# A two-layer decoder trunk on one core: scores of two heads in one bank, half projections with two banks, products of zeros ahead of three waits

## The chip, the core and the metric

The kernel runs on one core of a Trainium2 chip. TensorE (PE in the rows; its weight loads are PEld) multiplies, VectorE (DVE), ScalarE (ACT) and GpSimd (POOL) do the elementwise work, SyncE (SP) issues the loads. TensorE's clock is granted at one of two levels, 1.2 or 2.4 GHz; the profile prints the granted clock of a stretch as a share of 2.4 GHz, so 0.50 is the lower level throughout. The metric is device time in microseconds (us) of one execution; the kernel before has a median of 691.52 us over 3 runs (688.81 to 693.57).

## The reference, cut to what matters

256 tokens of width 1024 go through two layers, each a mixer and a squared-ReLU MLP (1024 to 4096 and back) with residual adds and RMSNorms, then a last RMSNorm. The change is in the second mixer, native sparse attention with 16 heads in 4 key/value groups; with 256 tokens every 64-token block is selected and the window covers all, so both of the branches below are causal attention over their own keys:

```python
q, k_c, v_c, k_s, v_s, k_w, v_w, gl = split(h @ w_in)     # h = rms_norm(x)
gates = sigmoid(gl)                                       # 16 heads x 3 branches
kc_blk, vc_blk = compress_blocks(k_c), compress_blocks(v_c)   # silu(blk @ w1) @ w2, 15 blocks
p_c = masked_softmax(q @ kc_blk.T);    o_c = p_c @ vc_blk
p_s = masked_softmax(rope(q) @ rope(k_s).T);  o_s = p_s @ v_s
p_w = masked_softmax(rope(q) @ rope(k_w).T);  o_w = p_w @ v_w
out = (g0 * o_c + g1 * o_s + g2 * o_w) @ w_out
x = x + out;  x = x + squared_relu(rms_norm(x) @ w_up) @ w_down
```

## The kernel before, in words

**Layout.** Activations lie as features x tokens: `X` is 128 x 8 x 256. Products are made at better than half precision by splitting both factors into a rounded part and a rest: a weight piece `st` (128 x 1024 or 128 x 560) is loaded, ScalarE rounds it into `uh`, VectorE subtracts to get `ul`, and every 128 x 128 block takes three products of 256 columns (`mm256`). Weights stream through 8 staging slots and 4 pairs of `uh`/`ul`.

**Order of the work.** Nothing here is left to a compiler's scheduler. Every piece of work is a Python generator that yields the engine, bank, flag or token that it wants next; the class `Order` keeps a clock for each engine and, at every step, lets the generator go on whose next instruction could start first by its own table of costs. The result is one fixed list of instructions for each engine, and on the chip each engine runs its list strictly in order. So a change of costs, banks or tile shapes anywhere in a stretch reorders that stretch on all engines.

**PSUM.** There are 8 banks of 128 x 512 floats. A generator that asks for a bank holds it until the evacuation has read it.

**The second mixer** (`layer1`) runs, by `ORDER1`, the key projection `kk` (tiles `KD`, `KL`), the first half of the queries `q0`, the keys of the compressed branch `kc`, the per-token projection `vg` (values and gates; the rows `b<-uh,x` and `b<-ul,x` with 280 columns), the compression `cmp` (rows `b<-st,blk`, fp32), the queries `q1` and the output projection `wo` (rows `b<-ohl,uh` and `b<-ohl,ul`). The head work is done in 8 units, called **pairs 0 to 7** here, each for two heads of two groups: `q0` brings pairs 0 to 3, `q1` pairs 4 to 7. A pair goes through

- `attend`: the rotary embedding and the split of the queries on VectorE and ScalarE (tiles `swq`, `qrot`, `qr`), then on TensorE the scores: for token block t=0 256 columns a head, for t=1 512 columns a head, each as a product with `KD`, one with `KL` and a mask product (`ngeb`). A head's scores have a bank of their own, four banks in all.
- `soften`: the maximum on VectorE (`nm`), the exponentials on ScalarE (`px`); `weigh` divides and gates them (`px<-px,den`).
- `turn` and `spread` (called by `combine`): TensorE transposes the weights (`b<-par,px`), they are copied out (`pts`) and multiplied with the values (`b<-pts,VT`); the compressed branch is added (`b<-pct,VCB`) and the sum split into `ohl`, which the output projection reads. The flag `o7` says that pair 7 is done.

`proj_tok` (line 612) makes all four 280-column accumulators of `vg` at once in four banks. `proj_out` (line 627) takes four banks at its start, goes through six of the eight feature blocks `k` with 24 products each as the `ohl` come, and finishes the last two block by block. `Norm.finish` (line 745) ends a norm: a sum over partitions on TensorE, a reciprocal root on VectorE, two transposes of a column.

The helper `call` (line 303) issues every engine instruction but DMAs, so nearly all rows name line 303; tiles tell them apart.

## Time and profile before

| | |
|---|---|
| median of 3 runs | 691.52 us |
| the profiled execution | 692.06 us, span 690.3 us |
| PE busy | 664.9 us, 96% of the span |
| PEld, DVE, ACT, POOL busy | 91%, 68%, 57%, 18% |
| mean granted clock | 0.985 |
| the chain that ended last | PE 81%, DVE 12%, ACT 3% |
| loads | 109.08 MB, 158 GB/s in the mean |

PE counts as busy while a product is under way, at either clock and however far its products lie apart, so 96% does not say that PE works at its full rate in 96% of the span. For that, the products in a stretch are counted against the distance at which the same kind of product starts in a stretch where PE waits for nothing. In the timeline a row gives start, duration, engine, operation and, in brackets, the idle time before it with the instruction that ended it; the ends of products are modelled, so the distance of two starts is the better price than the duration.

### The profile page before, as it was taken

To read this page: it belongs to the slowest core of one execution; us is meant where nothing else is said; L and a number is where in the kernel's file an instruction comes from. 1 tells how busy PE (TensorE), PEld (TensorE's weight loads), DVE (VectorE), ACT (ScalarE), POOL (GpSimd) and SP (SyncE) were. 2 spreads that over 40 slices of the span, in tenths; PEclk is the share of its full clock that TensorE was granted. 3 is DMA by queue.
4 is the path that set the end of the run, shared out by engine and by line. 5 is a ranking of instruction groups with operands and counts; after the bars stand their busy time and mean duration, and the time that the engine had idled before them with its cause. 6 is when DMAs were issued, how large, how long until landed. Compare 5 with 4: busy or idle time off the path is not lost.

```text
span 690.3 us, 16239 instructions
## 1 busy us (share of the span) xinstructions
PE 664.9 (96%) x6629; PEld 626.2 (91%) x6629; DVE 466.4 (68%) x869; ACT 392.7 (57%) x766; POOL 125.2 (18%) x172
## 2 busy tenths in 40 slices
PE   8999899999999999999999989998999999999994
PEld 5999799989999999999999847895799999999994
DVE  6999777686765565555589976895696565555452
ACT  7565232245887885444457566666588887644430
POOL 1001766311200000010122630030130000011121
PEclk9999999999999999999999979999999999999997
DMA  8861533135666666666644528140145555555401
GB/s 293 297 225 33 156 96 93 52 113 174 187 201 192 193 199 190 193 198 192 190 147 133 184 88 279 62 153 31 62 153 184 187 202 192 189 204 189 153 1 62
DMA packets 32330, 109.08 MB, mean 158 GB/s; under 512 B 3712, under 2 KB 3968, under 8 KB 32256
## 3 DMA queue, kind: packets, MB, share of 16 engines
q1 hardware_dynamic: 31968, 107.53, 49.2%
q8 instruction: 52, 0.85, 0.5%
q10 hardware_dynamic: 288, 0.52, 0.2%
q14 instruction: 22, 0.18, 0.1%
HBM read 106.99 MB, written 1.05 MB: 157 GB/s over the span
## 4 chain that ended last, share of the span: by engine, by line
PE 81%; DVE 12%; ACT 3%; issue 2%; DMA 1%; SPq 0%; DVEq 0%; ACTq 0%
PE b L303 81%; DVE ul L303 4%; DMA X<-xt 1%; ACT uh L303 1%; DVE nm L303 1%; DVE cvconv L303 1%; DVE kc L303 1%; DVE swq L303 1%; DVE rqt L303 1%; DVE lc L303 0%; ACT E L303 0%; DVE x L303 0%; SPq L435 0%; DVE preconv L303 0%; DVE al L303 0%
## 5 line engine op out<-in xcount | busy, mean ns | idle before, releaser
L303 DVE TENSOR_TENSOR ul<-st,uh 128x1024 fp32r<-128x1024 f32 (+3 forms) x204 | 242.1, 1190 | 153.1 <-ACT uh L303 150.9
L303 ACT ACTIVATE uh<-st 128x1024 fp32r<-128x1024 f32 (+3 forms) x204 | 206.1, 1012 | 199.1 <-PE b L303 179.0
L303 PE MATMUL b<-x,uh 128*128 128x256 f32 x1664 | 294.5, 280 | 1.6 <-ACT uh L303 0.9
L303 PEld LDWEIGHTS b<-x,uh 128*128 128x128 f32 x1664 | 251.8, 188 | 5.2 <-ACT uh L303 2.0
L303 PE MATMUL b<-x,ul 128*128 128x256 f32 x832 | 231.2, 278 | 1.2 <-DVE ul L303 1.1
L303 PE MATMUL b<-U,uh 128*128 128x256 f32 x1024 | 174.2, 276 | 0.0
L303 PEld LDWEIGHTS b<-x,ul 128*128 128x128 f32 x832 | 156.4, 188 | 2.4 <-DVE ul L303 2.4
L303 PEld LDWEIGHTS b<-U,uh 128*128 128x128 f32 x1024 | 154.1, 188 | 0.0
L303 PE MATMUL b<-U,ul 128*128 128x256 f32 x512 | 141.3, 276 | 0.0
L303 PEld LDWEIGHTS b<-U,ul 128*128 128x128 f32 x512 | 96.1, 188 | 0.0
L303 POOL TENSOR_TENSOR nacc<-nacc,sq 128x256 f32<-128x256 f32 x24 | 28.4, 1182 | 251.4 <-ACT sq L303 248.7
L303 ACT ACTIVATE px<-b,nm 128x128 f32<-128x128 f32 (+1 forms) x64 | 26.2, 422 | 7.6 <-DVE nm L303 7.5
L303 ACT ACTIVATE U<-u 128x256 fp32r<-128x256 f32 x64 | 26.8, 419 | 2.0
L303 ACT ACTIVATE u<-t 128x256 f32<-128x256 f32 x64 | 26.7, 418 | 2.0
L303 DVE TENSOR_TENSOR U<-u,U 128x256 fp32r<-128x256 f32 x64 | 27.0, 424 | 0.9 <-ACT U L303 0.9
L303 PE MATMUL b<-uh,x 128*128 128x264 f32 (+1 forms) x128 | 25.3, 291 | 0.0
L303 POOL TENSOR_TENSOR px<-px,den 128x128 f32<-128x128 f32 x32 | 15.1, 500 | 54.5 <-DVE den L303 53.6
L303 PE MATMUL b<-ohl,uh 128*128 128x256 f32 x128 | 24.0, 287 | 0.2
L303 POOL TENSOR_TENSOR X<-X,par 128x256 f32<-128x256 f32 x8 | 5.5, 693 | 99.3 <-ACT nacc L303 90.3
L303 ACT ACTIVATE t<-b 128x256 f32<-128x256 f32 x64 | 23.4, 365 | 0.0
L303 ACT ACTIVATE pts<-b 128x384 f32<-128x384 f32 x26 | 12.2, 490 | 17.6 <-PE b L303 17.5
L303 DVE TENSOR_REDUCE nm<-b 128x2 f32<-128x256 f32 (+1 forms) x32 | 16.6, 549 | 6.1 <-PE b L303 6.0
(269 smaller groups left out, 797.0 us busy)
## 6 DMA issues: line engine op xcount, KB each, us to landing
st<-wts SPq DMA_DIRECT2D x188, 512.0 KB, 4.1
st<-wts SPq DMA_DIRECT2D x8, 280.0 KB, 2.8
st<-wts SPq DMA_DIRECT2D x8, 264.0 KB, 5.9
st<-wts SPq DMA_DIRECT2D x8, 256.0 KB, 6.3
X<-xt SPq DMA_DIRECT2D x3, 256.0 KB, 6.4
par<-par SPq DMA_DIRECT2D x1, 525.0 KB, 5.8
out_dram<-X SPq DMA_DIRECT2D x2, 256.0 KB, 2.6
out_dram<-X ACTq DMA_DIRECT2D x2, 256.0 KB, 3.1
```

Of the source, the lines that this page charges most:

```text
L303: r = f(*a, **k)
```

## The change

Six edits; the first mixer, both MLPs and the loads keep their instructions.

1. **Scores of t=0 share a bank.** Both heads of a pair write 2 x 256 columns of one bank, only the first product clears it, and `soften2` takes one maximum over 512 columns instead of `soften`'s two over 256. t=1 keeps two banks.
2. **`KL` gets 128 rows.** It had, for each head, 64 rows (the rounding rest of the head's keys); now the other 64 rows are zeros, set once by two POOL memsets, and the product runs over all 128 rows of `qr`. The column counts are the same.
3. **`vg` in halves** (`proj_tok2`): the first 280 columns for both token blocks with two banks, then the second 280. The weight array is laid out to match; bytes and products are the same.
4. **`wo` in halves** (`proj_half`, since `HALF[1]` is 1): output features 0 to 511 with two banks over all eight `k`, then 512 to 1023 with two. It asks for its first bank only once the flag `o0` is up.
5. **Products of zeros** (`keep`): where the planner's clock sees PE idle for more than `KEEP` = 900 ns ahead of a pair's scores, a turn or the last norm's two products, it issues up to 8 products of a tile of zeros (128 x 512, bf16) into the bank that the waiting work is about to clear.
6. The 9 products at the start of the program become 11, on the same tile of zeros.

```diff
+WARM, KEEP, KMAX = 11, 900.0, 8
+ONE, WO, HALF, SOFT, TURN, VH = 1, 0, (0, 1), None, None, 1
...
+    def keep(bank):
+
+        gap = order.idle('PE', bank)
+        if gap > KEEP:
+            n = min(int((gap - 400) / 215), KMAX)
+            for _ in range(n):
+                nc.tensor.matmul(bank, e.zeros[:, :128], e.zeros, start=True, stop=True)
...
+    def proj_tok2(norm, half, finish):
+
+        for b in range(2):
+            accs = yield from banks(2)
+            for k in range(KT):
+                if k % 2 == 0:
+                    hi, lo = yield from unit()
+                yield 'flag', f'n{norm.idx}x{k}'
+                s = slice(k % 2 * half, k % 2 * half + half)
+                for t in range(2):
+                    yield 'PE'
+                    xt = norm.x[:, k, :, t * 128:t * 128 + 128]
+                    mm256(accs[t][:, :half], xt[:, 0], xt[:, 1], hi[:, s], lo[:, s], k == 0, k == KT - 1)
+            spawn(finish(accs, b))
...
+    def proj_half(x, ready, nxt):
...
+        for half in range(2):
+            accs = yield from banks(2)
...
+            for k in range(KT - 2):
+                yield from ready(k)
+                if k % 2 == 0:
+                    u = yield from unit()
+                for m in range(4):
+                    yield 'PE'
+                    piece(k, m, u)
+            for k in (KT - 2, KT - 1):
+                yield from ready(k)
+            u = yield from unit()
+            for m in range(4):
+                for k in (KT - 2, KT - 1):
+                    yield 'PE'
+                    piece(k, m, u)
+                if m % 2:
+                    spawn(evac(4 * half + m, accs[m // 2]))
...
             yield 'PE'
+            if self.last:
+                keep(ss)
...
-        KL = p1.tile([128, 2, 2, T], F32R, name="KL")
+        KL = p1.tile([128, 2, 2, 2, T], F32R, name="KL")
...
+            for s in range(2):
+                yield 'G'
+                G.memset(KL[64 - 64 * s:128 - 64 * s, s].bitcast(F32), 0.0)
+            flag('KL')
...
-                bk = yield from banks(2)
-                sc = [view(b, 2, n) for b in bk]
+                one = ONE and not t
+                if one:
+                    b = yield BANK
+                    bk, sc = [b, b], [view(b, 2, 2, n)[:, s] for s in range(2)]
+                else:
+                    bk = yield from banks(2)
+                    sc = [view(b, 2, n) for b in bk]
                 q = slice(t * 128, t * 128 + 128)
                 yield 'PE'
+                e.keep(bk[0])
                 for s in range(2):
-                    PE.matmul(sc[s], qr[:, s, q], KD[:, s, p, :, :n], start=True, stop=False)
+                    PE.matmul(sc[s], qr[:, s, q], KD[:, s, p, :, :n], start=not (one and s), stop=False)
                 yield 'PE'
                 for s in range(2):
-                    PE.matmul(sc[s], qr[own[s], s, q], KL[own[s], p, :, :n], start=False, stop=False)
+                    PE.matmul(sc[s], qr[:, s, q], KL[:, s, p, :, :n], start=False, stop=False)
...
+        def soften2(u, bank, PX, nm, den):
+
+            sc = view(bank, 2, 2, 128)
+            yield 'V'
+            V.tensor_reduce(nm[:, 0], sc, axis=AX.X, op=OP.max, negate=True)
...
+        yield 'flag', f'o{WO}'
+        yield from (e.proj_half if HALF[1] else e.proj_out)(lambda k: [ohl[k // 2][:, a, k % 2] for a in range(2)], ready, nxt)
```

The planner's list moves between the key projection and the start of the second MLP; before and behind that, only the 2 + 10 products of zeros at the two ends of the program are new. Three places matter for what follows.

TensorE's list, where the per-token projection ends and the scores of the next pair begin. Before, pairs 0 and 1 have had their scores among the `vg` products; then come four compression products, pair 2 and pair 3:

```order
L303 MATMUL b_5467<-uh_5569,x 128x280
L303 MATMUL b_5721<-st,blk_4976 64x256
L303 MATMUL b_5721<-st,blk_4977 64x256
...
L303 MATMUL b_5730<-KD,qr 128x256
L303 MATMUL b_5731<-KD,qr 128x256
L303 MATMUL b_5730<-KL,qr 128x256
...
L303 MATMUL b_5754<-KD,qr 128x256
```

The same place now; pair 0 has had its scores ahead of `vg`, and no score stands among the `vg` products:

```order
L314 MATMUL b_5584<-uh_5593,x 128x280
L420 LDWEIGHTS zeros
L420 MATMUL b_5690<-zeros 128x512
L314 MATMUL b_5690<-KD,qr 128x256 x2
L314 MATMUL b_5690<-KL,qr 128x256 x2
...
L314 MATMUL b_5709<-KD,qr 128x256 x2
...
L314 MATMUL b_5743<-st,blk_4978 64x256
...
L314 MATMUL b_5758<-par,px_0_5430 128x128
L314 MATMUL b_5758<-par,px_0_5431 128x128 x2
```

So two products of zeros, pairs 1 and 2, six compression products and then the first transposes follow the last `vg` product; pair 3's scores have moved behind 30 of the 32 compression products.

VectorE's list behind its last `ul` of `vg` (`ul_5570` before). Before, the query work of pairs 1, 2 and 3 alternates with maxima (`nm`) of scores that TensorE has yet to make:

```order
L303 TENSOR_TENSOR ul_5570<-st,uh_5569 128x560
L303 TENSOR_TENSOR kc<-b_5421,rbc 64x128 x2
L303 TENSOR_REDUCE nm<-b_5545 128x2
L303 STREAM_SHUFFLE swq<-QQ 128x256
...
L303 TENSOR_REDUCE nm<-b_5575 128x2
L303 TENSOR_REDUCE nm<-b_5608 128x2
L303 TENSOR_TENSOR qr<-qrot,qr 64x256 x2
...
L303 TENSOR_REDUCE nm<-b_5680 128x2
L303 TENSOR_REDUCE nm<-b_5681 128x2
L303 TENSOR_TENSOR qr<-qrot,qr 64x256 x2
L303 CAST qr<-qrot 64x256
```

Now pair 0's maxima lie ahead of the last `ul`, and the query work of pairs 1 and 2 follows it in one piece, `x4` being both pairs' halves:

```order
L314 TENSOR_TENSOR ul_5594<-st,uh_5593 128x560
L314 TENSOR_TENSOR kc<-b_5419,rbc 64x128 x2
L314 STREAM_SHUFFLE swq<-QQ 128x256
L314 TENSOR_TENSOR swq<-swq,rtab 128x256
L314 TENSOR_TENSOR qrot<-qrot,swq 128x256
...
L314 CAST qr<-qrot 64x256
L314 TENSOR_TENSOR qr<-qrot,qr 64x256 x4
L314 TENSOR_SCALAR gate<-gate 128x96
L314 TENSOR_REDUCE nm<-b_5690 128x4
```

TensorE's list at the end of the attention, where pair 7 is combined. Before, 144 of the 192 output products stand ahead of this place, 48 behind it:

```order
L303 MATMUL b_6748<-par,px_2_6466 128x128
L303 MATMUL b_6748<-par,px_2_6467 128x128 x2
L303 MATMUL b_6321<-ohl_6592,uh_6424 128x256 x2
...
L303 MATMUL b_6794<-pts,VT 64x128 x2
L303 MATMUL b_6794<-pct,VCB_4971 128x256
L303 MATMUL b_6318<-ohl_6804,uh_6474 128x256 x2
```

Now 72 stand ahead of it, since the second half may not begin before the first has ended, and 120 behind:

```order
L314 MATMUL b_6308<-ohl_6518,uh_6276 128x256 x2
L314 MATMUL b_6308<-ohl_6518,ul_6277 128x256
L314 MATMUL b_6689<-par,px_3_6562 128x128
...
L314 MATMUL b_6688<-pts,VT 64x128 x2
L314 MATMUL b_6688<-pct,VCB_4973 128x256
L314 MATMUL b_6307<-ohl_6709,uh_6321 128x256 x2
```

So the attention of pairs 5 to 7 has half as many output products among its own, and a longer tail of them follows.

## Rows read from the trace of the kernel before

**Rows 1.** Windows by stage: length, busy us (count) per engine, granted clock, DMA

```profile
core 0: us, PE busy (x) PEld busy (x) DVE busy (x) ACT busy (x) POOL busy (x), PEclk, DMA share, GB/s
354.40:379.80 25.40, 25.40 (x224) 25.40 (x225) 23.62 (x43) 17.51 (x34) 7.79 (x7) 1.00 0.40 122
379.80:397.70 17.90, 17.27 (x122) 14.91 (x121) 16.93 (x42) 10.29 (x30) 11.31 (x20) 1.00 0.51 177
397.70:413.20 15.50, 13.24 (x56) 6.25 (x55) 11.63 (x31) 9.21 (x38) 5.55 (x12) 0.67 0.23 72
413.20:450.30 37.10, 37.10 (x305) 29.63 (x304) 27.45 (x75) 24.53 (x72) 4.25 (x6) 1.00 0.49 169
450.30:502.60 52.30, 48.34 (x362) 39.47 (x361) 37.21 (x89) 30.11 (x88) 10.23 (x20) 0.97 0.25 81
502.60:514.80 12.20, 11.61 (x99) 11.16 (x97) 11.47 (x14) 9.85 (x19) 5.42 (x5) 1.00 0.56 171
```

**Rows 2.** Timeline of TensorE, from the end of `vg` to the first transposes

```profile
398.04 1.08 PE L303 MATMUL b<-st,blk 128*64 128x256 f32 x8 [0.33 <-issue]
400.96 0.81 PE L303 MATMUL b<-KD,qr 128*128 128x256 f32 x2 [1.84 <-DVE qr L303]
...
409.07 3.68 PE L303 MATMUL b<-st,blk 128*64 128x256 f32 x16
412.68 0.64 PE L303 MATMUL b<-par,px 128*128 128x128 f32 x3
```

**Rows 3.** Timeline of VectorE, behind the last `ul` of `vg`

```profile
388.99 1.13 DVE L303 TENSOR_TENSOR ul<-st,uh 128x560 fp32r<-128x560 f32 x1
390.16 0.60 DVE L303 TENSOR_TENSOR kc<-b,rbc 64x128 f32<-64x128 f32 x2
...
391.25 0.45 DVE L303 STREAM_SHUFFLE swq<-QQ 128x256 f32<-128x256 f32 x1
...
392.54 1.28 DVE L303 TENSOR_REDUCE nm<-b 128x2 f32<-128x512 f32 x2
393.85 0.87 DVE L303 TENSOR_TENSOR qr<-qrot,qr 64x256 fp32r<-64x256 f32 x2
```

**Rows 4.** Timeline of TensorE, prices at full clock: compression, transposes, products with the values

```profile
422.75 0.65 PE L303 MATMUL b<-st,blk 128*64 128x256 f32 x4
423.34 0.87 PE L303 MATMUL b<-par,px 128*128 128x128 f32 x6
424.14 1.91 PE L303 MATMUL b<-pts,VT 128*64 128x256 f32 x16
```

**Rows 5.** Timeline of TensorE, the scores of pair 4 and the start after them

```profile
443.22 0.39 PE L303 MATMUL b<-KD,qr 128*128 128x256 f32 x2
...
444.00 0.71 PE L303 MATMUL b<-KD,qr 128*128 128x512 f32 x2
444.65 0.50 PE L303 MATMUL b<-KL,qr 64*128 64x512 f32 x2
445.08 0.39 PE L303 MATMUL b<-ngeb,identb 128*128 128x256 bf16 x2
445.31 0.98 PE L303 MATMUL b<-KCB,QQ 128*128 128x32 f32 x8
```

**Rows 6.** Timeline of TensorE, waits in the attention of pairs 5 to 7 and behind it

```profile
468.68 0.52 PE L303 MATMUL b<-par,px 128*128 128x128 f32 x3 [2.35 <-ACT px L303]
...
511.92 0.39 PE L303 MATMUL b<-x,uh 128*128 128x256 f32 x1 [0.46 <-DVE x L303]
```

**Rows 7.** Timeline of GpSimd, the rotary table of the second mixer

```profile
355.33 1.31 POOL L303 TENSOR_TENSOR rope<-rtab,rbc 128x512 f32<-128x512 f32 x1 [7.62 <-ACT rbc L303]
```

**Rows 8.** Timeline of TensorE, start of the program and the last norm

```profile
1.22 4.02 PE L303 MATMUL b<-warm 128*128 128x512 bf16 x9 [1.22 <-DVE warm L303]
...
10.61 0.50 PE L303 MATMUL b<-x,uh 128*128 128x256 f32 x2 [0.75 <-ACT uh L303]
...
683.08 0.69 PE L303 MATMUL b<-par,ncol 128*128 128x128 f32 x2 [1.82 <-DVE ncol L303]
```

More of the change, by code (lines that the diff above doesn't have):

```diff
@@ L75, in _layout @@
     eo = i['ev_w_out'][0].reshape(2, 4, 128, 1024)
-    for h in (1, 0):
-        chunks.append(eo[h].transpose(1, 0, 2).reshape(128, CH))
+    if HALF[0]:
+        a = eo[::-1].reshape(8, 128, 2, 512).transpose(2, 1, 0, 3)
+        chunks.extend(a.reshape(2, 128, CH))
+    else:
+        chunks.extend(eo[h].transpose(1, 0, 2).reshape(128, CH) for h in (1, 0))
     def mlp(l):
@@ L101, in _layout @@
     wo = i['od_w_out'][0].reshape(2, 2, 4, 64, 1024).transpose(2, 0, 1, 3, 4).reshape(1024, 1024)
-    part['wo'] = [h.transpose(1, 0, 2).reshape(128, CH) for h in wo.reshape(2, 4, 128, 1024)]
+    part['wo'] = [h.transpose(1, 0, 2).reshape(128, CH) for h in
+                  (wo.reshape(8, 128, 2, 512).transpose(2, 0, 1, 3) if HALF[1] else wo.reshape(2, 4, 128, 1024))]
     for k in ORDER1:
@@ L225, in spend, with idle @@
         c.last = eng
+    def idle(self, eng, bank):
+        c = self.cur
+        start = max(c.hold + self.IN[eng], c.t + self._lag(c, eng))
+        return start - max(self.free[eng], self.since[id(bank)] + self.IN[eng])
     def later(self, ns):
@@ L398, in _build @@
     ones = const.tile([128, 1], F32, name="ones")
+    e.zeros = const.tile([128, 512], BF16, name="zeros")
+    def keep(bank):
[4 more added lines that the diff above has]
+                nc.tensor.matmul(bank, e.zeros[:, :128], e.zeros, start=True, stop=True)
+            at = int(order.free['PE'] / TICK)
+            order.cols[at] = order.cols.get(at, 0.0) + n * 512
+    e.keep = keep
     def begin():
@@ L766, in finish @@
             yield 'PE'
+            if self.last:
+                keep(rb)
             for t in range(2):
@@ L1426, in ready @@
                 yield 'flag', 'ya1'
-        yield from e.proj_out(lambda k: [y[:, k % 4] for y in (yb if k < 4 else ya)], ready, nxt)
+        yield from (e.proj_half if HALF[0] else e.proj_out)(lambda k: [y[:, k % 4] for y in (yb if k < 4 else ya)], ready, nxt)
 def layer1(e, n, nxt):
@@ L1666, in attend @@
                     PE.matmul(sc[s][:, :, n - 128:], e.identb, e.ngeb[:, None, :].to_broadcast([128, 2, 128]),
-                              start=False, stop=True)
-                    spawn(soften(u, s, t, bk[s], sc[s], PX, nm, den))
+                              start=False, stop=not one or s == 1)
+                    if not one:
+                        spawn(soften(u, s, t, bk[s], sc[s], PX, nm, den), SOFT)
+                if one:
+                    spawn(soften2(u, bk[0], PX, nm, den))
             give('qr')
@@ L1681, in soften @@
             flag(f'px{u}.{s}{t}')
+        def soften2(u, bank, PX, nm, den):
+            sc = view(bank, 2, 2, 128)
+            yield 'V'
+            V.tensor_reduce(nm[:, 0], sc, axis=AX.X, op=OP.max, negate=True)
+            for s in range(2):
+                for b in range(2):
+                    yield 'A'
+                    A.activation(PX[0][:, s, b], sc[:, s, b], AF.Exp, bias=nm[:, 0, s, b:b + 1],
+                                 accum_out=den[:, 0, s, b:b + 1])
+                flag(f'px{u}.{s}0')
+            release(bank)
         def weigh(i, p, PX, den):
@@ L1866, in ready @@
             yield 'flag', f'o{k}'
-        yield from e.proj_out(lambda k: [ohl[k // 2][:, a, k % 2] for a in range(2)], ready, nxt)
+        yield 'flag', f'o{WO}'
+        yield from (e.proj_half if HALF[1] else e.proj_out)(lambda k: [ohl[k // 2][:, a, k % 2] for a in range(2)], ready, nxt)
 def kernel(**inputs):
```

57 lines of the change are left out of this document (42 added, 15 removed).

## The prediction

> **What bounds the kernel now.** I began with the windows by stage, because 96% PE busy hides more than it tells. [rows 1] Outside the second mixer PE starts a 256-column product every 25.40/224 = 0.113 us and waits for nothing; there the change alters nothing, so its worth is read between 379.8 and 514.8 us. I count each stage's products at the distance of their starts in undisturbed stretches: a pair's scores 445.31 - 443.22 = 2.09 us [rows 5]; a compression product (423.34 - 422.75)/4 = 0.148 us, a transpose (424.14 - 423.34)/6 = 0.133 us, a value product 1.91/16 = 0.119 us [rows 4].
>
> - The per-token stage, 17.90 us, is 0.63 us short of busy and holds two pairs' scores (4.2), so its 96 products took (17.90 - 0.63 - 4.2)/96 = 0.136 us each, 13.1 in all.
> - The 15.50 us behind it hold 28 compression products (4.1), two pairs (4.2) and three transposes (0.4): 8.7 us of work, **6.8 us lost**. Its granted clock is 0.67, the lowest of the table.
> - 413.2 to 450.3 us is full, at clock 1.00: nothing to win.
> - The output stage, 52.30 us: 192 products (21.8), three pairs (6.3), 48 transposes (6.4), 64 value products (7.6), and 20 small ones at a transpose's price (2.7), 44.8 us; **7.5 us lost**, 4.0 of it open idle time.
> - The first 96 products of the second MLP: 12.20 us for 10.9, **1.3 us lost**.
>
> The timeline of TensorE shows how the 6.8 us go [rows 2]: `vg` ends, eight compression products fill one us, PE waits 1.84 us for the `qr` of pair 2, and then the clock is at its lower level until the transposes: pairs 2 and 3 with four compression products take 409.07 - 400.96 = 8.1 us, where 4.2 + 0.6 would do. `qr` is late because VectorE is nearly full (16.93 of 17.90 us [rows 1]) and its list puts query work behind maxima [rows 3].
>
> **The change, part by part.**
>
> *Order around `vg` and the compression.* Pair 0's scores come first, so `vg` starts 2.1 us later, at 381.9, and without other scores among its products ends at 381.9 + 13.1 = 395.0. VectorE's last `ul` ended at 390.1; counting both lists from the rotary table on with the traced durations puts it 0.4 later, at 390.5. Then come a `kc` couple (0.60), the query work of pairs 1 and 2 in one piece, 392.54 - 391.25 = 1.29 each [rows 3], a cast (at most half of the 0.87 for two halves, 0.43) and two `qr` halves (0.87): pair 1 is ready at 390.5 + 0.6 + 2.6 + 0.4 + 0.9 = 395.0, pair 2 at 395.9. PE's wait shrinks from 2.2 us to about 0.5, and the clock has no long idle stretch to fall in. From there to the start of the work that followed 413.2 the same products are due, two pairs at 4.2 instead of 8.1 less 0.6. What is late next: the copies of the first transposes, on ScalarE behind pair 1's exponentials and on VectorE behind pair 3's query work; PE waits about 0.9 us for them in my walk through the three lists. Of 0.63 + 6.8 = 7.4 us lost, 1.4 stay: **-6.0**. Bounds: -7.4 (no wait is left) and -1 (the clock falls all the same).
>
> *Shared bank.* One maximum over 512 columns (1.28/2 = 0.64 us [rows 3]) for two over 256, on VectorE, saves less than one of 0.64 a pair; it is in the walk.
>
> *`KL` over 128 rows.* At t=1 the two 64-row products take 445.08 - 444.65 = 0.43 us, the two full `KD` products of the same width 444.65 - 444.00 = 0.65 [rows 5]. If full rows cost what `KD` costs, 8 pairs pay 8 x 0.22 = **+1.8**; the lower bound is 0. I take the upper, being nearest in shape. The Trainium skill's page "TensorE: Matmul & The Clock Gate" (Part 3: Packing small matmuls) says that products on different rows of the array run at once; filling the rows gives that up, which speaks against this edit. By that rule t=0, half as wide, would lose half as much too, and the term would be +2.7. The two memsets stand ahead of `rope`, where POOL was idle for 7.62 us [rows 7]: nothing, unless they take longer than that.
>
> *`vg` in halves.* Products and bytes are the same, two banks are free earlier: 0 beyond the walk.
>
> *`wo` in halves.* Before pair 7 is combined, 72 output products instead of 144 are at hand; the other 72 x 0.113 = 8.2 us move behind it. In exchange four banks fewer are tied up, and the scores of a pair's t=1 follow its t=0 directly. Walked through with traced durations, pairs 4 to 7 leave PE waiting about 1.0 us for pair 4's weights, 1.6 for copies behind exponentials on ScalarE, 0.9 for pair 5's weights and 2.0 in smaller pieces: 5.5 against 7.5 lost now, **-2.0**, bounds -5 and +6 (three quarters of the 8.2 turn into waits). The wait of 2.35 us for `px` [rows 6] is what this trades against. Behind it `X` of the first half is ready 96 products before the end, 10.9 us early, so the MLP's first products no longer wait for `x` (0.46 of the 1.3 [rows 6]; the rest was slowed): **-1.3**, bounds -1.3 and 0.
>
> *Products of zeros.* At the start they cost 4.02/9 = 0.45 us each [rows 8]; two stand before pair 1 inside its wait, two more at the start are paid back at the first wait behind them (0.75 us [rows 8]) but for 0.15. At the end, five lie in a gap of 1.82 us [rows 8]: 5 x 0.45 = 2.25 would delay the two transposes by 0.4, and if their clock is held they gain up to 0.3. Taken as 0.
>
> Sum: -6.0 + 1.8 - 2.0 - 1.3 = -7.5, from the profiled execution's 692.06 to 684.6. That execution lies 0.5 over the median of 691.52, so the median to expect is **684.1**.
>
> **The rivals.**
>
> *The clock falls anyway.* The `keep` rule acts where the planner sees idle time, not where the chip has it; only two products stand in the mixer. If VectorE is later than counted by 1.5 us, PE idles 2 us at 395 as it does now at 399, and pairs 1 and 2 run at the lower clock: 8.1 - 4.8 = +3.3, twelve compression products at (412.68 - 409.07)/16 = 0.23 us [rows 2] instead of 0.148, +1.0, and the wait itself 0.5: 689. For: VectorE's durations swing when POOL works beside it. Against: query work now stands in one piece.
>
> *Starved attention.* Half of the 8.2 us becomes waiting: instead of -2.0 it is +4, 690. For: lists run strictly in order, and the wait of 2.35 us arose with twice the filler. Against: 2 banks more.
>
> *Slower than before.* The starved attention also loses the clock. From pair 5's transposes to pair 7's end PE has some 20 us of work (two pairs' scores 4.2, 36 transposes 4.8, 48 value products 5.7, 36 output products 4.1, small ones). At the lower clock work took 8.1/4.8 = 1.7 times as long [rows 2]: +14, and with the -2.0 not had, 700. It decides once more than about 18 us of that work runs at the lower level. Against: the output stage had a wait of 2.35 us and still a granted clock of 0.97 [rows 1], 3 us of low clock at most. [...]
>
> *Upside.* All waits of both stages vanish: -7.4 - 5 - 1.3 + 1 = -12.7, near 679.
>
> **How the numbers follow.** What a measurement of this kernel tells from no change is about 1%, 6.9 us: faster is below 684.6, slower above 698.4. The forecast has 0.62 and spreads over 680.5 to 687.5, six tenths of it below 684.6; the upside 0.07; the fallen clock 0.16; starved attention 0.09; slower 0.06, nearly all of it over 698.4. So faster is 0.62 x 0.6 + 0.07 = 0.44, slower 0.05, the same 0.51. A range of 679.5 to 691.0 leaves out the slower case, the worse part of the starved one and the best of the upside.
>
> **What would show it.** In the profile after: the granted clock of the compression stage near 1.00 instead of 0.67, and a wait of under 1 us before the second pair's scores; the t=1 `KL` products at the distance of the `KD` ones; waits for `px` and `pts` between the output products' start and pair 7, 5 to 6 us in sum; 120 output products in a row, and no wait for `x` behind them; the last transposes no later than now. The prediction is wrong if the clock drops at the same place, if the sum of waits in the output stage exceeds 8 us, or if a stage that I hold for unchanged moves.

## The result, and the profile after

The changed kernel has a median of 683.39 us over 4 runs (682.36 to 683.91), the kernel before on the same chip 692.55 over 4 (688.81 to 695.13): a ratio of 0.987, 95% interval 0.9821 to 0.9919. 684.1 had been forecast. The two sums agree better than their terms do, and the terms are what this part is about.

The windows by stage of the changed kernel, to be read against [rows 1]: the per-token stage, pairs 1 and 2 with the compression, the stretch to the first output product, the output stage, the entry of the MLP.

```profile
core 0: us, PE busy (x) PEld busy (x) DVE busy (x) ACT busy (x) POOL busy (x), PEclk, DMA share, GB/s
380.28:397.54 17.26, 16.03 (x123) 15.24 (x121) 16.42 (x40) 11.65 (x33) 7.97 (x14) 1.00 0.48 158
397.54:416.35 18.81, 17.08 (x131) 10.84 (x129) 16.51 (x38) 13.14 (x45) 9.50 (x18) 1.00 0.59 188
416.35:446.97 30.62, 30.26 (x245) 26.15 (x245) 26.23 (x75) 19.05 (x61) 2.71 (x6) 1.00 0.39 146
446.97:496.29 49.32, 47.14 (x362) 39.23 (x361) 38.13 (x87) 30.93 (x91) 12.71 (x21) 1.00 0.28 86
496.29:508.50 12.21, 12.21 (x110) 12.21 (x109) 9.55 (x23) 9.01 (x18) 3.92 (x3) 1.00 0.56 180
```

The granted clock is 1.00 in every row; before it was 0.67 in one stage and 0.97 in another. PE still has open waits in four of the rows, and VectorE is still nearly full in the per-token stage (16.42 of 17.26 us).

To see where the time went, I took starts of TensorE's products that stand at the same place of both programs: the second norm's sum, the last product of the first MLP, the first output product, the first and the last product of the second MLP. In the kernel before they are at 181.95, 346.17, 450.33, 502.62 and 678.89 us; in the timeline of the changed one:

```profile
183.98 0.58 PE L314 MATMUL b<-ones,nacc 128*128 128x1 f32 x4 [0.30 <-DVE nacc L314]
348.15 0.28 PE L314 MATMUL b<-U,ul 128*128 128x256 f32 x1
446.97 0.39 PE L314 MATMUL b<-ohl,uh 128*128 128x256 f32 x2
496.29 0.39 PE L314 MATMUL b<-x,uh 128*128 128x256 f32 x2
671.00 0.28 PE L314 MATMUL b<-U,ul 128*128 128x256 f32 x1
```

| stretch between these starts, us | before | after | difference | forecast |
|---|---|---|---|---|
| start to the second norm (first mixer) | 181.95 | 183.98 | +2.03 | 0 |
| first MLP | 164.22 | 164.17 | -0.05 | 0 |
| second mixer to the first output product | 104.16 | 98.82 | -5.34 | -6.0 + 5/8 x 1.8 = -4.9 |
| output stage | 52.29 | 49.32 | -2.97 | -2.0 + 3/8 x 1.8 = -1.3 |
| second MLP | 176.27 | 174.71 | -1.56 | -1.3 |
| from there to the end of the span | 11.41 | 11.10 | -0.31 | 0 |
| span | 690.3 | 682.1 | -8.2 | -7.5 |

The first row is no work of the change. In the first mixer, whose instructions are the same, TensorE stands still for longer, 2.62 us instead of 1.81, and the granted clock from 84 to 95 us is 0.84 instead of 1.00. The timeline of TensorE before:

```profile
86.27 0.25 PE L303 MATMUL b<-tt,al 32*32 32x32 f32 x4 [1.81 <-issue]
```

After:

```profile
86.72 0.32 PE L314 MATMUL b<-tt,al 32*32 32x32 f32 x6 [2.62 <-issue]
```

The wait is put down to "issue": nothing that the profile shows released it. So the changed stretches are worth about 10 us in this pair of profiles, and 2 us of that are hidden by the first mixer.

The first stage in question, TensorE around the end of the per-token projection and at the last transposes ahead of pair 3, to be read against [rows 2]:

```profile
385.47 0.37 PE L314 MATMUL b<-uh,x 128*128 128x280 f32 x1 [1.23 <-DVE kc L314]
...
397.54 0.61 PE L420 MATMUL b<-zeros 128*128 128x512 bf16 x2
398.83 0.84 PE L314 MATMUL b<-KD,qr 128*128 128x256 f32 x2 [0.68 <-DVE qr L314]
...
403.11 1.52 PE L314 MATMUL b<-st,blk 128*64 128x256 f32 x12
...
415.17 1.25 PE L314 MATMUL b<-pts,VT 128*64 128x256 f32 x8 [0.86 <-ACT pts L314]
```

PE waits for a new reason, 1.23 us for a bank that `kc` still holds, in the fourth `vg` product; then 398.83 - 397.54 = 1.29 us pass until pair 1 starts (0.61 of zeros, 0.68 open). The two pairs behind it take 403.11 - 398.83 = 4.28 us, at full clock, where before pairs 2 and 3 and four compression products took 8.1. (The timeline counts two products for each compression product of the lists: these x12 are its six.)

The scores of pair 4 in the changed kernel, which answer to [rows 5]:

```profile
440.08 0.39 PE L314 MATMUL b<-KD,qr 128*128 128x256 f32 x2
440.31 0.39 PE L314 MATMUL b<-KL,qr 128*128 128x256 f32 x2
440.54 0.39 PE L314 MATMUL b<-ngeb,identb 128*128 128x256 bf16 x2
440.69 0.71 PE L314 MATMUL b<-KD,qr 128*128 128x512 f32 x2
441.25 0.63 PE L314 MATMUL b<-KL,qr 128*128 128x512 f32 x2
441.71 0.39 PE L314 MATMUL b<-ngeb,identb 128*128 128x256 bf16 x2
441.94 0.98 PE L314 MATMUL b<-KCB,QQ 128*128 128x32 f32 x8
```

A pair takes 441.94 - 440.08 = 1.86 us, before it took 2.09: **0.23 less, where 0.22 more had been forecast**. At t=0 the `KL` products went from 443.86 - 443.54 = 0.32 to 0.23 and the `KD` products ahead of them from 0.32 to 0.23; at t=1 `KD` went from 0.65 to 0.56, `KL` from 0.43 to 0.46. The products of t=0 in the kernel before, and the weight loads of their `KL`:

```profile
443.54 0.39 PE L303 MATMUL b<-KL,qr 64*128 64x256 f32 x2
443.86 0.39 PE L303 MATMUL b<-ngeb,identb 128*128 128x256 bf16 x2
...
443.54 0.19 PEld L303 LDWEIGHTS b<-KL,qr 64*128 64x128 f32 x2
```

The weight loads of the same products in the changed kernel:

```profile
440.20 0.30 PEld L314 LDWEIGHTS b<-KL,qr 128*128 128x128 f32 x2
```

Before, the two 64-row products of a pair did run at once: by their records they start 3 to 4 ns apart, in all eight pairs and at both t, where the full-row ones of pair 4 start 0.11 us (t=0) and 0.23 us (t=1) apart. But their weight loads begin only when the products do (443.54 and 443.54); those of the full rows begin 0.11 us ahead of their products (440.20 and 440.31), while the `KD` products still run. So what the two heads win by running at once is lost again around them: 0.64 us from the first `KD` to the mask at t=0, where full rows one after the other take 0.46.

The open waits of the output stage, against [rows 6], and the transposes of the last norm, against [rows 8]:

```profile
456.83 0.52 PE L314 MATMUL b<-par,px 128*128 128x128 f32 x3 [0.92 <-ACT pts L314]
...
463.89 0.38 PE L314 MATMUL b<-ohl,uh 128*128 128x256 f32 x1 [0.75 <-ACT ohl L314]
464.44 0.39 PE L314 MATMUL b<-ohl,uh 128*128 128x256 f32 x1 [0.17 <-DVE ohl L314]
...
675.19 0.43 PE L314 MATMUL b<-par,ncol 128*128 128x128 f32 x2 [0.73 <-DVE ncol L314]
```

In the output stage these are 1.84 us of open waits, none for `px`; all idle time of the stage is 49.32 - 47.14 = 2.18 us, before it was 4.0. In the MLP behind it PE no longer waits for `x`. Before, this stage also held a stretch at the lower clock, behind the wait of 2.35 us for `px` [rows 6]:

```profile
465.30:475.30 10.00, 6.66 (x38) 4.43 (x37) 6.77 (x21) 5.90 (x19) 1.65 (x4) 0.83 0.03 12
```

A mean of 0.83 over 10 us is 3.4 us at the lower level; the three other profiles with the order of the kernel before have 0.83 at this place too, the changed kernel's have 1.00.

### The profile page after: what moved, and what is told of

Its sections match the earlier page's. It is cut to its first block, busy times and chain, and to the rows that moved or that the text cites. A ratio compares the mean times of both kernels' runs of the same rounds, so it can differ in the third digit from the quotient of the medians.

```text
span 682.1 us, 16243 instructions
## 1 busy us (share of the span) xinstructions
PE 660.3 (97%) x6643; PEld 627.9 (92%) x6643; DVE 463.8 (68%) x867; ACT 389.7 (57%) x761; POOL 127.1 (19%) x173
## 4 chain that ended last, share of the span: by engine, by line
PE 78%; DVE 13%; ACT 3%; issue 2%; DMA 2%; SPq 0%; DVEq 0%; ACTq 0%
PE b L314 78%; DVE ul L314 4%; DMA st<-wts 2%; ACT uh L314 1%; DVE nm L314 1%; DVE qr L314 1%; DVE cvconv L314 1%; DVE swq L314 1%; ACT px L314 1%; DVE kc L314 1%; DVE lc L314 0%; ACT E L314 0%; DVE rqt L314 0%; DVE qrot L314 0%; SPq L461 0%
## 5 line engine op out<-in xcount | busy, mean ns | idle before, releaser
L314 PEld LDWEIGHTS b<-ohl,uh 128*128 128x128 f32 x128 | 19.6, 188 | 2.4 <-ACT ohl L314 1.3
L314 PEld LDWEIGHTS b<-uh,x 128*128 128x128 f32 x128 | 20.3, 188 | 1.4 <-issue 1.4
```

Of the source, the lines that this page charges most:

```text
L314: r = f(*a, **k)
```

## The experiments

All are compared by the same stretches. "To output" runs from the last product of the first MLP to the first output product, "first mixer" from the first norm's sum to the second's; both are starts of rows in each profile. The kernels were timed in four batches, each beside the kernel before, and medians are compared closely only within one: the result above; b_kl128, a_kl64t1, a_nozero and a_half00 (kernel before 693.20 us); b_again, b_kl128_2, a_vh0 and a_one0 (691.66); a_again, a_nozero_2 and a_klp3 (692.58). Across batches the ratios to the kernel before are compared; the changed kernel's are 0.987 and, for a_again, 0.986 (0.983 to 0.989). `b_` names are made from the kernel before, `a_` names from the changed one.

| profile | median us (runs) | first mixer | to output | output stage | second MLP |
|---|---|---|---|---|---|
| before | 692.55 (4) | 163.30 | 104.16 | 52.29 | 176.27 |
| b_again | 690.48 (1) | 163.63 | 101.36 | 52.70 | 176.28 |
| b_kl128 | 689.14 (12) | 167.11 | 98.98 | 52.39 | 176.26 |
| b_kl128_2 | 690.32 (1) | 165.58 | 100.81 | 52.24 | 176.26 |
| changed | 683.39 (4) | 165.98 | 98.82 | 49.32 | 174.71 |
| a_again | 682.84 (6) | 166.26 | 98.06 | 49.31 | 174.70 |
| a_kl64t1 | 683.17 (6) | 164.42 | 98.26 | 49.34 | 174.70 |
| a_nozero | 682.38 (5) | 165.28 | 97.12 | 49.30 | 174.70 |
| a_nozero_2 | 682.60 (6) | 166.77 | 97.99 | 49.27 | 174.70 |
| a_half00 | 686.97 (6) | 163.60 | 98.19 | 51.68 | 176.29 |
| a_vh0 | 684.00 (6) | 162.97 | 100.65 | 47.87 | 174.70 |
| a_one0 | 685.17 (7) | 165.29 | 99.77 | 50.40 | 174.71 |
| a_klp3 | 680.30 (6) | 163.70 | 101.27 | 43.08 | 174.70 |

**Full `KL` rows alone, in the kernel before (b_kl128).**

```diff
-                    PE.matmul(sc[s], qr[own[s], s, q], KL[own[s], p, :, :n], start=False, stop=False)
+                    PE.matmul(sc[s], qr[:, s, q], KL[:, s, p, :, :n], start=False, stop=False)
```

> The kernel before with one edit: KL gets 128 rows with zeros and its products run over all of them; TensorE's list is otherwise the same. Theory A (a 64-row product between 128-row products pays a change of shape at both of its ends): a pair's scores, from its first product to the one behind its last mask product, go from 2.09 us to about 1.80, as in the changed kernel; 8 pairs give -2.3 us, the stage after the per-token one keeps its low clock, and the time is near 690 (ratio 0.997). Theory B (the prediction: full rows cost what the KD products cost, 0.22 us more a pair): +1.8 us, near 694, and the t=1 KL products stand 0.65 us ahead of the mask instead of 0.43.

Measured: 689.14 against 693.2, ratio 0.9954 (0.9933 to 0.9975). Faster, so theory B fell. The t=1 scores of pair 4 in its timeline:

```profile
442.48 0.71 PE L303 MATMUL b<-KD,qr 128*128 128x512 f32 x2
443.03 0.63 PE L303 MATMUL b<-KL,qr 128*128 128x512 f32 x2
443.50 0.39 PE L303 MATMUL b<-ngeb,identb 128*128 128x256 bf16 x2
```

0.55 for `KD` and 0.47 for `KL` at t=1, as in the changed kernel, though nothing else was changed. One part of theory A failed too: it expected the low clock to stay, and the stretch to the output fell by 5.2 us, more than five pairs at 0.23 can give, while the output stage, with three pairs of its own, stayed at 52.39 us (its waits grew). TensorE's wait for `qr` was there, 1.53 us ahead of the third pair, but the clock did not follow. The window of 5 us behind that wait:

```profile
405.60:410.60 5.00, 5.00 (x36) 2.84 (x35) 4.90 (x13) 4.73 (x19) 3.26 (x6) 1.00 0.06 6
```

So two things had to be told apart: full rows, and the chance of one execution.

**Second profiles of the kernel before and of b_kl128 (b_again, b_kl128_2).**

> The kernel before, unchanged: a second profile of it. Theory A (the low clock behind the wait for the third pair's qr belongs to this order with 64-row KL products): the stage behind the per-token projection shows a granted clock near 0.67 again, and the second mixer takes about 156.5 us from the last product of the first MLP to the first of the second, as in the first profile. Theory B (whether the clock falls at that wait differs from one execution to the next): here it may stay at 1.00, and the mixer then takes about 153 us.

> The kernel before with 128-row KL products, a second profile. Its first one had the same two waits there as the kernel before (0.65 and 1.53 us where that had 0.33 and 1.84) and a clock of 1.00. Theory A (full rows keep the clock): 1.00 again, second mixer near 151.4 us. Theory B (chance): the clock can be low here, the mixer near 155.

Of the kernel before again, TensorE's wait ahead of the third pair:

```profile
401.38 0.81 PE L303 MATMUL b<-KD,qr 128*128 128x256 f32 x2 [1.85 <-DVE qr L303]
```

and the two windows of 5 us behind it:

```profile
403.20:408.20 5.00, 5.00 (x21) 2.21 (x20) 4.71 (x13) 4.72 (x19) 3.23 (x6) 0.66 0.00 0
408.20:413.20 5.00, 5.00 (x44) 2.93 (x42) 2.15 (x8) 1.59 (x5) 2.32 (x7) 1.00 0.60 219
```

The same wait of 1.85 us, and the clock is back at 1.00 after a few microseconds; in the first profile it had stayed at 0.50 for ten. b_kl128_2 waited 1.85 us too, and its clock fell:

```profile
402.28 0.81 PE L303 MATMUL b<-KD,qr 128*128 128x256 f32 x2 [1.85 <-DVE qr L303]
...
403.80:408.80 5.00, 5.00 (x22) 2.88 (x20) 4.49 (x13) 4.69 (x20) 2.71 (x6) 0.69 0.00 0
```

So of four profiles with this order, the three with waits of 1.84 to 1.85 us lost the clock, for 10 us once and for 3 to 4 us twice, and the one with 1.53 did not. Full rows do not keep the clock by themselves: theory A on b_kl128_2 fell. The length of the low stretch differs between executions, for which theory B holds, and the stretch to the output goes from 98.98 to 104.16 us with it.

Which of the two lengths is the usual one, the times of the kernel before tell, since each comes with its mean granted clock. Beside the experiments it ran 40 times. In 27 of these the clock is 0.986 or lower, as in the first profile (0.985), with a median of 693.2 us; in 9 it is 0.989 or higher, as in b_again (0.989), with a median of 689.5 us. So the long low stretch is nearer to the usual execution than the short one, as far as a mean over the whole program can say.

**64 rows again at t=1 (a_kl64t1).**

```diff
-                    PE.matmul(sc[s], qr[:, s, q], KL[:, s, p, :, :n], start=False, stop=False)
+                    r = own[s] if t else slice(0, 128)
+                    PE.matmul(sc[s], qr[r, s, q], KL[r, s, p, :, :n], start=False, stop=False)
```

> The changed kernel, but the KL products of t=1 (two banks) use the 64 rows that are not zero; t=0 keeps 128 rows. The lists are the same. Theory A (change of shape): t=1 goes back to 0.65 + 0.43 + 0.23 = 1.31 us a pair from 0.55 + 0.47 + 0.15 = 1.17, +0.14 a pair, +1.1 us in all, near 684.5. Theory B (full rows cost more): 0.22 a pair is saved, -1.8 us, near 681.6.

683.17 us, between the changed kernel's 682.84 and 683.39: the time tells nothing. Pair 2 in its timeline tells more:

```profile
401.61 0.72 PE L314 MATMUL b<-KD,qr 128*128 128x512 f32 x2
402.25 0.50 PE L314 MATMUL b<-KL,qr 64*128 64x512 f32 x2
402.69 0.39 PE L314 MATMUL b<-ngeb,identb 128*128 128x256 bf16 x2
```

`KD` is at 0.64 again and `KL` at 0.44: 1.08 against 0.56 + 0.46 = 1.02 in the changed kernel. The `KD` products are the same in both kernels; what they lose, 0.08 to 0.09 us, comes with the 64-row products behind them. What remains of a gain at `KL`, its own change back included, is 0.02 to 0.03. Theory B's 0.22 is not there, and theory A's 0.14 is 0.06: the mask product did not change, it had merely another follower in the rows that I compared.

**No products of zeros in the mixer and at the last norm (a_nozero, a_nozero_2).**

```diff
-            for _ in range(n):
+            for _ in range(0):
                 nc.tensor.matmul(bank, e.zeros[:, :128], e.zeros, start=True, stop=True)
```

> The changed kernel without the products of zeros ahead of the second pair (2) and at the last norm (5 and 5); the 11 at the start and all lists stay. Theory A (they hide nothing, as the prediction took them): TensorE's open wait before the second pair grows from 0.68 to about 1.3 us, the granted clock of that stage stays at 1.00, the start of the scores does not move, and the last transposes are up to 0.3 us later; within 0.5 us of the changed kernel. Theory B (they hold the clock): without them the clock falls at that wait as it did in the kernel before, pairs 1 and 2 take about 3.6 x 1.7 = 6.1 us instead of 3.6, the first twelve compression products 2.8 instead of 1.5: 3 to 4 us slower, near 687.

> The changed kernel without the products of zeros ahead of the second pair and at the last norm, a second profile. Theory A (they neither hold the clock nor cost anything): the stretch before the first output product lies anywhere between 97 and 99 us, the clock is 1.00. Theory B (they cost 1 us or more, by delaying the second pair or what follows it): 97.1 again. Theory C (they hold the clock, and the first profile without them was lucky): a low clock behind the wait for qr, 100 us or more.

682.38 and 682.60 us, ratios of 0.985 and 0.986 to the kernel before: nothing lost. TensorE's wait ahead of pair 1 in the first of the two:

```profile
398.41 0.75 PE L314 MATMUL b<-KD,qr 128*128 128x256 f32 x2 [1.19 <-DVE qr L314]
```

and its windows from the last `vg` product on:

```profile
397.20:402.20 5.00, 3.81 (x23) 2.83 (x22) 4.74 (x12) 2.59 (x11) 3.07 (x6) 1.00 0.08 31
402.20:407.20 5.00, 5.00 (x43) 3.26 (x42) 4.83 (x15) 5.00 (x25) 3.08 (x8) 1.00 0.43 122
```

An open wait of 1.19 us (1.22 in the second profile), and the clock stays at 1.00 both times. At this wait the clock holds without the zeros. The two profiles take 97.12 and 97.99 us to the output, the changed kernel's two 98.82 and 98.06, so that they cost something can't be told from the spread of executions.

**The changed kernel again (a_again).**

> The changed kernel, unchanged, a second profile on the chip of the two other runs. Both theories: 683.4 us, granted clock 1.00 from the per-token projection to the second MLP, second mixer 148 us give or take 1; the first mixer's stalls of TensorE without a releaser (2.62 us at the longest in the first profile) between 1.5 and 2.7 us. Theory A (the 1.7 us less of the kernel without products of zeros is a difference of executions): here the stretch before the first output product can take as little as its 97.1 us. Theory B (the products of zeros cost it): 98.2 or more again.

682.84 us; 98.06 us to the output, and in the first mixer a longest wait of 1.56 us instead of 2.62. Over all thirteen profiles the first mixer takes 162.97 to 167.11 us with the same instructions. The changed kernel's order had the clock at 1.00 from the end of the per-token stage to the second MLP in each of its six profiles (this one, the first, a_kl64t1, the two without zeros, and a_half00, whose order differs only behind the first output product).

**Output projection over four banks (a_half00).**

```diff
-ONE, WO, HALF, SOFT, TURN, VH = 1, 0, (0, 1), None, None, 1
+ONE, WO, HALF, SOFT, TURN, VH = 1, 0, (0, 0), None, None, 1
```

> The changed kernel with the output projection of the second mixer over four banks at once, as before, all else as changed. Theory A (the prediction: the halves save 2.0 us in the attention of the last pairs and 1.3 at the entry of the MLP): about 3.3 us slower than the changed kernel, near 686.7, with waits for px among the last pairs and for x in the MLP. Theory B (the gain of the output stage comes from the other edits, which also shorten a pair's scores and free banks): the stage from the first output product to the MLP stays within 1 us of its 49.3 us, and only the entry of the MLP loses about 1.5; near 685.

Rows of TensorE's timeline, of the last pair and of the MLP's first products:

```profile
480.23 1.90 PE L420 MATMUL b<-zeros 128*128 128x512 bf16 x8 [0.31 <-DVE ohl L314]
483.89 1.36 PE L314 MATMUL b<-par,px 128*128 128x128 f32 x9 [1.76 <-POOL px L314]
...
504.30 0.38 PE L314 MATMUL b<-x,uh 128*128 128x256 f32 x1 [0.42 <-DVE x L314]
```

686.97 us, ratio to the kernel before 0.9915 (0.9882 to 0.9949): +2.4 us in the output stage, +1.58 in the MLP, the wait for `px` and the wait for `x` are back. Theory A holds, with its sizes. One thing came along: with four banks the planner puts eight products of zeros ahead of the last transposes, so the kernel's own work pauses from 480.23 to 483.89, 3.66 us. The clock stays at 1.00 there, where the kernel before lost it behind a wait of 2.35 us; whether these zeros held it was not tried.

**Per-token projection over four banks (a_vh0), a bank for each head at t=0 (a_one0).**

```diff
-ONE, WO, HALF, SOFT, TURN, VH = 1, 0, (0, 1), None, None, 1
+ONE, WO, HALF, SOFT, TURN, VH = 1, 0, (0, 1), None, None, 0   # a_vh0
+ONE, WO, HALF, SOFT, TURN, VH = 0, 0, (0, 1), None, None, 1   # a_one0
```

> The changed kernel with the per-token projection over four banks at once, as before. Its list has two pairs' scores among the per-token products again and pairs 2 and 3 behind four compression products, as in the kernel before, but no products of zeros there. Theory A (the halves, by the order that they bring, are what shortened the wait for qr): the wait before the third pair returns, 1.5 to 2 us, and the stretch from the last product of the first MLP to the first output product takes 2 us more than the 98.8 of the changed kernel; near 685.5. Theory B (the order is worth little, and full KL rows keep the clock): that stretch stays within 1 us of 98.8; near 683.5.

> The changed kernel with a bank for each head at t=0 again (KL over 128 rows, halves as changed). Theory A (the shared bank saves a maximum a pair on VectorE and a bank, as the prediction held it worth little by itself): within 1 us of the changed kernel, near 684. Theory B (the bank and the maxima are what lets pair 0 go ahead and the halves work): 2 us more before the first output product and 1 to 2 more behind it, near 686.5.

a_vh0: 684.00 us, ratio to the kernel before 0.989 (0.9856 to 0.9924), which overlaps the changed kernel's 0.986. By its profile it loses 1.8 us before the output and wins 1.45 in the output stage; the mixer as a whole takes 148.52 us, the changed kernel's 148.14 and 147.37. Neither theory saw that: planner and banks shift work over the border between the stretches, and by the time `vg` in halves is worth too little to be told. The wait for `qr` that theory A expected did not come back; three waits for `kc` of 1.22, 1.06 and 0.92 us did its part, and the clock fell among them. A window of each of the two profiles, a_vh0 first, then a_one0:

```profile
384.00:391.00 7.00, 5.68 (x23) 5.41 (x24) 6.62 (x18) 4.80 (x18) 3.52 (x10) 0.51 0.00 1
386.80:390.30 3.50, 3.50 (x18) 3.50 (x17) 3.39 (x8) 1.48 (x5) 3.00 (x7) 0.51 0.27 92
```

In a_one0 it fell behind waits for `kc` of 1.60 and 1.06 us. Neither list has products of zeros in the mixer. So neither profile prices its edit by the order alone: a part of what each loses before the output is low clock, and one profile does not tell whether that comes every time.

a_one0: 685.17 us, ratio 0.991 (0.9878 to 0.9943), and 99.77 + 50.40 = 150.17 us for the mixer, 2.0 to 2.8 more than with the shared bank, about half on either side of the first output product. By the prediction's ratio of 1.7 the 3.5 us of low clock are about 1.4 us of that, an estimate. Nearer to theory B, but the intervals of the ratios overlap here too.

**A version that beats both (a_klp3).** VectorE is nearly full in the per-token stage, so one step was taken off it.

```diff
-            yield 'V'
+            KE = G if m == 3 else V
+            yield 'G' if m == 3 else 'V'
             for s in range(2):
-                V.tensor_sub(KL[own[s], s, m // 2, m % 2], t[own[s]], KD[own[s], s, m // 2, m % 2].bitcast(F32))
+                KE.tensor_sub(KL[own[s], s, m // 2, m % 2], t[own[s]], KD[own[s], s, m // 2, m % 2].bitcast(F32))
```

> The changed kernel with the subtraction that makes KL of the last key block on GpSimd instead of VectorE (two of 64 x 256, 1.02 us on VectorE in the changed kernel, right ahead of the kc rows for which TensorE waits 1.23 us in the fourth per-token product); the planner then orders that stretch anew and issues no products of zeros before the second pair. Theory A (VectorE's list is what bounds the stretch from the per-token projection to the first transposes): the kc wait shrinks by about 1 us and the qr wait with it, 1.5 to 2.5 us less before the first output product, near 681.5. Theory B (GpSimd is slower at it and shares its port with VectorE, and the new order finds another wait): within 1 us of the changed kernel either way, near 683.4.

680.30 us, ratio to the kernel before 0.9827 (0.9798 to 0.9857), where the changed kernel on the same chip has 0.9860 (0.9830 to 0.9890). The intervals overlap; the six times of each, 678.36 to 681.93 and 680.73 to 683.54 us, hardly do. The mixer by the trace is 144.35 us against 147.37 and 148.14. The wait that I had aimed at did not move, and the stretch to the end of `vg` did not either; the gain lies behind it. The wait for `kc` in its timeline:

```profile
383.83 0.37 PE L314 MATMUL b<-uh,x 128*128 128x280 f32 x1 [1.22 <-DVE kc L314]
```

VectorE's timeline at the same place of the changed kernel:

```profile
383.51 1.81 DVE L314 TENSOR_TENSOR kc<-b,rbc 64x128 f32<-64x128 f32 x6
385.35 1.02 DVE L314 TENSOR_TENSOR KL<-kst,KD 64x256 fp32r<-64x256 f32 x2
```

Its windows, the stretch from the end of `vg` to the first output product and the output stage:

```profile
395.80:447.79 51.99, 50.96 (x406) 40.26 (x406) 47.98 (x127) 39.30 (x131) 14.52 (x26) 1.00 0.43 161
447.79:490.87 43.08, 41.70 (x330) 36.15 (x328) 31.93 (x71) 24.60 (x67) 9.41 (x16) 1.00 0.25 87
```

GpSimd takes 1.63 us for what took VectorE 0.85 to 1.02, but nobody waits for it. The aim was misread: in the changed kernel that subtraction starts at 385.35, behind the six `kc` rows (383.51 to 385.32) whose end lets the product go on at 385.47, and not ahead of them as the expectation says, so to move it could not shorten this wait. The planner filled VectorE's freed time with further `kc` rows (ten in one piece instead of six). It also laid six pairs' scores and 60 transposes of weights ahead of the first output product instead of five and 48, and the two last stretches take 51.99 + 43.08 = 95.07 us where the changed kernel needs 496.29 - 397.54 = 98.75. Theory A's place was wrong, theory B's "another wait" did not appear; that a better order of the attention made the gain is read from the two lists and the windows, not tried by itself.

## Why the prediction was right, and which of its steps were not

The total, the sign and the range held. By its own steps:

- **Order around `vg`, -6.0: the clock part held, the wait part did not.** No low clock is left behind `vg`. Pairs 1 and 2 take 4.28 us where 4.2 had been counted, by luck: their products come to 2 x 1.86 = 3.72 at the price measured here, and 0.56 are pauses among them. PE's wait there is 1.29 us and not 0.5: VectorE's last `ul` ended at 394.62 (393.88 + 0.74), when 390.5 + 2.0 (the start of that stage lies 2.0 later in this execution) had been counted. And the `kc` rows that the new list puts ahead of `vg` brought a wait of 1.23 us that I had not listed. The open waits of this stretch do not shrink in sum, 1.23 + 0.68 + 0.86 + 0.32 = 3.1 us against 0.40 + 0.22 + 0.33 + 1.84 = 2.8; what it won is nearly all clock: the order of the kernel before with full rows, in the one profile in which its clock stayed at 1.00 (b_kl128), takes 98.98 us to the output, only 0.2 to 0.9 more than the changed kernel's two. How much that is depends on the execution it is compared with: the profile that I priced from had ten microseconds of low clock, a second one of the same kernel three to four, and their stretches differ by 104.16 - 101.36 = 2.8 us. The term was sized on the longer of the two, which by the granted clock of 40 further executions is nearer to the usual one. Less five pairs' `KL` at 0.23, 1.15 us, the stretch won 5.34 - 1.15 = 4.2 us between the first two profiles, and 3.2 us between the means of two profiles each, (104.16 + 101.36)/2 and (98.82 + 98.06)/2: the term was 1.8 to 2.8 us too large.
- **`KL`, +1.8: wrong in sign.** "If full rows cost what `KD` costs" took 0.65 us as the price of two 128-row products. That distance holds 0.09 us that come with the 64-row products behind them; with full rows behind them they take 0.56, and `KL` over full rows 0.46. By the distances the measured term is 8 x -0.23 = -1.8. By the time full rows alone are worth 0.46% (0.25 to 0.67), 1.7 to 4.6 us; the two agree, but the time does not single out the products, since the clock behind the `qr` wait moved as well and the output stage of that kernel did not get shorter. The range for it had ended at 0 below, since I knew no row that showed a change of row count by itself. The `KD` products at t=0 carried the same surcharge, 0.32 us instead of 0.23. The Trainium skill's page "TensorEngine Tiling (Array Packing)" (Tiling Modes, Key Properties) says that a change of tiling mode drains TensorE, without a price. The 0.09 us would fit that; the trace shows the weight load of the 64-row products starting only with them, and whether the time goes to a drain or to that load no run tells apart. The Trainium skill's page "TensorE: Matmul & The Clock Gate" (Part 3: Packing small matmuls), which the prediction cites, says that products on different rows run at once, and the trace agrees: they start 3 to 4 ns apart. The +2.7 us that the prediction drew from it did not come, since running at once did not pay for the border: in a_kl64t1 the 64 rows at t=1 cost 0.06 us a pair more than full rows, where by the prediction they would have cost 0.22 less.
- **The shared bank, "in the walk": mis-sized.** Undone alone it costs 2.0 to 2.8 us in the mixer by one profile, of which about 1.4 are low clock. That it frees a bank and a maximum a pair all through the stretch, which a walk over three lists at one place did not show, is the likely reason; no run separates the two.
- **`wo` in halves, -2.0: held**, as far as it can be singled out. Undone it costs 2.4. The stage won 2.97, which is 2.3 less three pairs at 0.23; but full rows alone did not shorten the stage of the kernel before (52.24 and 52.39 us against 52.29 and 52.70), and some of the 2.97 is the 3.4 us of low clock that the changed kernel does not have there, about 1.4 us by the prediction's ratio of 1.7, an estimate. The counted sum of losses was right too (44.8 us of work less 3 x 0.23 leaves 5.2 of 49.32, and 5.5 were forecast), but only 1.84 of it are open waits; the rest is products that start late without an idle row. The point "waits for `px` and `pts`, 5 to 6 us" was therefore wrong as a sign to look for.
- **MLP entry, -1.3: held**, -1.56, and undone +1.58.
- **Zeros, 0: held** in the mixer. The price of 0.45 us was one of the start of the program: two took 0.61 us in the mixer, and the delay of 0.4 us at the last norm did not come, since its transposes start 4.19 us behind the last MLP product in both kernels. At the last norm the transposes finish sooner, 675.66 - 675.19 = 0.47 us to the copy behind them instead of 0.72, though two of the six profiles without zeros at this place had 0.47 and 0.49 as well. For the start nothing is settled: the first norm comes at 18.00 instead of 18.65, and over all profiles either kind lies anywhere from 17.3 to 19.3.
- **"A stage that I hold for unchanged moves"** was named as a sign of error, and the first mixer did, by +2.0 us against the change. It is the spread of executions, so the sign was badly chosen.

So the forecast of the total was near by luck in part: in the pair of profiles `KL` was 3.6 us too dear, and against that stand an order term 1.8 us too large and the first mixer's 2.0 us, which is no work of the change; the other terms were within 0.3. Of the rivals, the fallen clock and the starved attention did not come; the clock of the output stage is 1.00.

What stays open: why the same wait of 1.85 us costs 3 us of low clock in one execution and 10 in the next. How much of the range from 688.81 to 695.13 of the kernel before that explains is known only in the main: over its 40 further executions the time falls as the mean clock rises, from 692.0 to 695.3 us at 0.981 to 687.4 us at 0.993, but the mean does not say in which stage the clock was low.

## What to carry to other kernels

The distance of two starts is a price only for the pair of shapes that it stands between: before pricing a product by it, find the same product with a neighbour of its own shape, and look whether the weight load starts ahead of the product or with it. A stage with a low granted clock should be profiled a second time before its loss is put into a sum, since here the wait repeated and the length of the low stretch did not; the mean clock that comes with each timed execution then says which profile is the usual one. Where a planner lays out the lists, freeing an engine at one place moves other work there; measure the whole stage and not the wait that was aimed at.

## What the runs showed of the hardware that was not expected

- Two 64-row products between 128-row ones are dearer than two 128-row products with half of the rows zero: 0.32 + 0.32 us for `KD` and `KL` of 256 columns against 0.23 + 0.23 (b_kl128 and the changed kernel), 0.65 + 0.43 against 0.56 + 0.46 of 512. The 64-row ones run at once, but their weight loads start only with them.
- Ahead of the scores behind `vg` the granted clock stayed at 1.00 through open waits of 1.19, 1.22 and 1.53 us, and fell behind waits of 1.84 and 1.85 us in all three profiles that had them. The length of one wait does not decide it elsewhere: among the `vg` products a wait of 1.22 us was followed by no low clock in the changed kernel's profiles, and in a_vh0, with waits of 1.06 and 0.92 us behind it, by 6.8 us of it; in the first mixer the clock fell behind 1.56 us in a_again and stayed behind 2.20 us in b_again. The Trainium skill's page "TensorE: Matmul & The Clock Gate" (Part 1: The HAM clock gate) holds that the number of slow products at the start of one and the same kernel varies from run to run. For a wait in the middle of a kernel these runs show the like: 10 us of the lower level once and 3.4 us twice behind the same wait.
- TensorE's waits without a releaser among the 32 x 32 products of the first mixer, 2.2 to 4.1 us in sum, differ from one execution to the next by as much as single edits of this change are worth.
